# A hybrid decoder layer: low parts of the last head on GpSimd, and the level of 16 block by block

## The chip, the cores and the metric

The kernel runs on one core of one Trainium2 chip. The metric is the device time of one execution in microseconds (us). A core has five engines with an instruction queue each: TensorE (PE, matrix multiplies; its weight loads are shown apart as PEld), VectorE (DVE), ScalarE (ACT), GpSimd (POOL) and SyncE (SP, which here issues the DMA transfers). The engines work at the same time and wait for one another through semaphores; each takes its own instructions in the order in which they stand. Operands lie in SBUF, the on-chip memory of 128 partitions; matrix products land in PSUM, eight banks of 512 float32 columns.

## The reference, cut to what matters

One decoder layer over 2048 tokens of width 1024: a normed projection feeds four heads of a gated linear recurrence (HGRN2) and eight heads of sliding-window attention; both are joined by an output projection, and a gated MLP follows. All is float32.

```python
u = rmsnorm(h, norm_mix_w[l])
proj = u @ w_in[l]
...
f = lb + (1.0 - lb) * jax.nn.sigmoid(hf.astype(jnp.float32))
...
    scores = jnp.einsum('bhtk,bhsk,bhtsk->bhts', qi, ki, decay)
    intra = jnp.einsum('bhts,bhsv->bhtv', scores, vi)
...
m = jnp.maximum(jnp.max(scores, axis=-1, keepdims=True), sink)
p = jnp.exp(scores - m)
denom = jnp.sum(p, axis=-1, keepdims=True) + jnp.exp(sink - m)
...
mix = jnp.concatenate([o_hg, o_att], axis=-1)
h = h + mix @ w_out[l]
```

## The kernel before

**Products in three parts.** A float32 operand x is kept as a high part (a cast to float32r by ACT) and a low part (x minus the high part, one subtraction with two SBUF inputs). A product is then high by high, high by low and low by high: three PE instructions. `split` (line 214) makes the parts of an activation tile, XH and XL; `prep` (line 177) loads a weight tile and makes whi and wlo; `unit` (line 190) multiplies a weight tile with eight activation tiles over two blocks of 512 tokens, 48 matrix instructions. Before the change ACT makes every high part and DVE every low part.

**Stages.** The 2048 tokens go in two halves of 1024. In each half four rounds (`h` = 0 to 3, line 1106 on) run one head of the recurrence (`hgrn`, line 433) and two heads of attention (`attend`, line 343) side by side. Then come the output projection (`out_proj`, line 641), the gate and up products and the down projection. This study is about the last round (`h` = 3) of each half, called **the last head** here. It has no projections of other heads left to fill PE. In their place the output projection already begins: while the last head's recurrence and attention are computed, the mix tiles 0, 4, 1, 5, 2 and 6 (three of the recurrence, `hg` tiles; three of attention, `att` tiles) are split, and the products `pop` of output tiles 0, 1 and 2 run with the six tiles that exist; tiles 7 and 3 are this round's own results and come last.

**Attention of the last head.** q (`att` tile 3) is split for two key/value groups and two blocks of 512 tokens: ACT casts qh (lines 359, 360), DVE makes ql (line 361), four times 64x512. PE makes the scores psc, ACT and DVE move and mask them into sc (lines 378 to 381), DVE takes the maximum (384), ACT the exponentials (394), DVE scales (399), PE transposes (ppt, 408), DVE masks (po, pp, 411), PE multiplies with the values (poT, 419).

**The recurrence by levels.** The decayed scores inside a chunk of 128 tokens are built by levels m = 1, 2, 4, ... 64: at each level PE multiplies K and Q (plev), DVE multiplies Q and K by the decays f (lines 522, 523) for the next level, and the level's scores are placed in the matrix ST. A level therefore waits for the one before it: plev, then Q and K, then the next plev. For m below 32 the last head computes a level as eight products of a whole chunk (line 515) of which the wanted blocks are picked by a predicated copy with a mask on DVE (line 538); for m = 32 and 64 each block is a small product of its own (line 520) and ACT copies it into place (line 543). After the last level come the transposes pkn, the state updates pu and SS, and the outputs po. In the round before, `hgrn` ends with a chain of tiny DVE instructions of 128x8 (lines 158 to 168, an inverse square root) that feeds the scaling `on` (587), PE's transposes pot (592), the product with the gate (593) and the next head's PSUM banks; this chain of the third head falls into the beginning of the last head.

**Order.** Instructions are not issued as the code is written: a scheduler at build time lays all engines' instructions out in order of its own estimate of time, so a change of one duration or engine reorders the neighbours. The order of each engine is then fixed; on the chip only waits move things. GpSimd has nothing to do before the change but the masks at the start. The pools that matter: PSUM has two banks of the kind `hg` (plev, pot, pdiag, pkn, pu, po) and two of `at` (psc, ppt, poT).

Of the kernel before, what the change touches and what calls it, by code (L numbers as in the profile page):

```python
# [8 lines left out]
F32 = mybir.dt.float32  # L9
# [4 lines left out]
ALU = mybir.AluOpType  # L14
# [4 lines left out]
D = 1024  # L19
# [6 lines left out]
HG = 4  # L26
ATT_J = 4
# [22 lines left out]
def hymba_layer(ctx: ExitStack, tc: tile.TileContext, a: dict, out: bass.AP):  # L50
    nc = tc.nc
# [122 lines left out]
            nc.sync.dma_start(t, src)  # L174
        return t

    def prep(src, slots=False, parts=(slice(0, D),), between=[]):

        raw = raw4(None)
        hi, lo = [hp.tile([P, D], F32R, tag="m", name=f"w{t}", bufs=KT) if slots else  # L180
                  wp.tile([P, D], F32R, tag=t, name=f"w{t}", bufs=2) for t in ("hi", "lo")]
        for c in parts:
            nc.sync.dma_start(raw[:, c], src[:, c])
            nc.scalar.copy(hi[:, c], raw[:, c])  # L184
            nc.vector.tensor_tensor(lo[:, c], raw[:, c], hi[:, c].bitcast(F32), op=ALU.subtract)  # L185
            if between:
                between.pop(0)()
        return hi, lo
# [26 lines left out]
    def split(src, w=None, eng=None, dst=None):  # L215

        h, l = dst or new_x()
        if w is None:
            nc.scalar.copy(h, src)
            (eng or nc.vector).tensor_tensor(l, src, h.bitcast(F32), op=ALU.subtract)  # L220
        else:
            nc.scalar.activation(h, src, AF.Identity, scale=w)
            nc.vector.scalar_tensor_tensor(l, src, w, h.bitcast(F32), op0=ALU.mult, op1=ALU.subtract)
        return h, l
# [118 lines left out]
    def attend(hf, j, X, invb, KS, V, mix, p):  # L343
# [8 lines left out]
        for g in range(NB):  # L352
            sc = p.tile([P, 2, 4, P], F32, tag="sc", name="sc", bufs=2)
            gs = slice(g * 512, (g + 1) * 512)
            for kv in range(2):
                r, other = rows(kv), rows(1 - kv)

                qh, ql = [p.tile([P, 512], F32R, tag="pp", name=n, bufs=4) for n in ("qh", "ql")]
                nc.scalar.copy(qh[r], qT[r, gs])
                nc.scalar.copy(qh[other], qT[r, gs])  # L360
                nc.vector.tensor_tensor(ql[r], qT[r, gs], qh[r].bitcast(F32), op=ALU.subtract)
                nc.scalar.copy(ql[other], ql[r].bitcast(F32))
                for i0 in (0, 2):
                    pb = ps("at", "psc")
                    first = hf == 0 and g == 0 and i0 == 0
                    for i in range(2):
                        n = g * 4 + i0 + i
                        w0 = 1 if first and i == 0 else 0
                        o = pb[:, i * 256 + w0 * P:(i + 1) * 256]
                        ks = slice((n + w0) * P, (n + 2) * P)  # L370
                        for t, qx in enumerate((qh, ql)):
                            nc.tensor.matmul(o, qx[:, (i0 + i) * P:(i0 + i + 1) * P], KS[:, kv, ks],
                                             start=t == 0, stop=t == 1)
                    pv = pb.rearrange("p (i w k) -> p i w k", i=2, w=2)
                    dst = sc[:, kv, i0:i0 + 2]
                    if first:
                        nc.vector.memset(dst[:, 0], NEG)
                        nc.scalar.copy(dst[:, 1], pv[:, 1, 0])
                    else:
                        nc.scalar.copy(dst, pv[:, :, 0])  # L380
                    nc.vector.copy_predicated(
                        dst, C.own.bitcast(U32).unsqueeze(1).to_broadcast([P, 2, P]), pv[:, :, 1])
            m = p.tile([P, 2, 4], F32, tag="mx", name="m", bufs=2)
            nc.vector.tensor_reduce(m.rearrange("p a b -> p (a b)"),
                                    sc.rearrange("p a b c -> p (a b) c"), axis=AX.X, op=ALU.max)
            sk = C.sinkb[:, j].unsqueeze(2).to_broadcast([P, 2, 4])
            nc.vector.tensor_tensor(m, m, sk, op=ALU.max)
            es = p.tile([P, 2, 4], F32, tag="es", name="es", bufs=2)
            nc.vector.tensor_tensor(es, sk, m, op=ALU.subtract)
            nc.vector.tensor_scalar(m, m, -1.0, None, op0=ALU.mult)  # L390
            den = p.tile([P, 2, 4], F32, tag="den", name="den", bufs=2)
            for kv in range(2):
                for i in range(4):
                    nc.scalar.activation(sc[:, kv, i], sc[:, kv, i], AF.Exp, bias=m[:, kv, i:i + 1],
                                         accum_out=den[:, kv, i:i + 1])
            nc.scalar.activation(es, es, AF.Exp)
            nc.vector.tensor_tensor(den, den, es, op=ALU.add)
            nc.vector.reciprocal(den, den)
            nc.vector.tensor_tensor(sc, sc, den.unsqueeze(3).to_broadcast([P, 2, 4, P]), op=ALU.mult)
            scs.append(sc)  # L400
# [32 lines left out]
    def hgrn(hf, h, X, invb, vs, WG, mix, p, fu=None):  # L433
# [51 lines left out]
        def place_pairs():  # L485
# [14 lines left out]
            ov = odd[r].rearrange("p r (b m) -> p r b m", m=m)  # L500
            return lambda: nc.vector.copy_predicated(STv[r, :, 1, :, 1], mk[r], ov)

        for m in LEVELS:
            nb = HALF // (2 * m)
            nbc = 64 // m
            Qv = Q.rearrange("p (b w m) -> p b w m", w=2, m=m)
            Kv = K.rearrange("p (b w m) -> p b w m", w=2, m=m)
            Fv = F.rearrange("p (b w) -> p b w", w=2)
            pl = ps("hg", "plev")
            paired = m < 32 and h < HG - 1  # L510
            if paired:
                pairs()
            elif m < 32:
                for c in range(TT):
                    marks[m] = nc.tensor.matmul(pl[:, c * 64:(c + 1) * 64], K[:, c * P:(c + 1) * P],
                                                Qv[:, c * nbc:(c + 1) * nbc, 1], start=True, stop=True)
            else:
                for c in range(TT):
                    for s0 in range(0, P, 2 * m):
                        nc.tensor.matmul(pl[s0:s0 + m, c * m:(c + 1) * m], K[:, c * P + s0:c * P + s0 + m],  # L520
                                         Q[:, c * P + s0 + m:c * P + s0 + 2 * m], start=True, stop=True)
            nc.vector.tensor_tensor(Qv[:, :, 1], Qv[:, :, 1], Fv[:, :, 0:1].to_broadcast([P, nb, m]), op=ALU.mult)
            done = nc.vector.tensor_tensor(Kv[:, :, 0], Kv[:, :, 0], Fv[:, :, 1:2].to_broadcast([P, nb, m]), op=ALU.mult)
            if left:
                with tc.issue_after(done.ins):
                    left()
                left = None
            if m < 64:
                nc.vector.tensor_tensor(Fv[:, :, 0], Fv[:, :, 0], Fv[:, :, 1], op=ALU.mult)
                F = Fv[:, :, 0]  # L530
            else:
                F = p.tile([P, nb], F32, tag="F", name="F", bufs=2)
                nc.vector.tensor_tensor(F, Fv[:, :, 0], Fv[:, :, 1], op=ALU.mult)
            if paired:
                left = place_pairs()
            elif m < 32:
                mk = C.lmask[m].bitcast(U32).rearrange("p (b m) -> p b m", m=m)
                nc.vector.copy_predicated(ST.rearrange("p c (b w m) -> p c b w m", w=2, m=m)[:, :, :, 1],
                                          mk.unsqueeze(1).to_broadcast([P, TT, nbc, m]),
                                          pl.rearrange("p (c b m) -> p c b m", c=TT, m=m))  # L540
            else:
                for s0 in range(0, P, 2 * m):
                    nc.scalar.copy(ST[s0:s0 + m, :, s0 + m:s0 + 2 * m],
                                   pl[s0:s0 + m, 0:TT * m].rearrange("p (c m) -> p c m", c=TT))
# [101 lines left out]
    def out_proj(hf, M, p):  # L646
# [6 lines left out]
        ops = Operands(p)  # L653
        ops.get("B11", 0)
        kept, v = [], []
        W = [prep(a["w_out"][d], d == 2) for d in range(3)]
        first = None
        xs = []
        for d in range(KT):
# [443 lines left out]
    for hf in range(NH):  # L1103
        X, kv, invb, rs, f0 = nxt
        with ExitStack() as st:
# [5 lines left out]
            for h in range(HG):  # L1111
# [3 lines left out]
                if h == HG - 1:  # L1115
                    next(at)
                    next(hg)
                    for kt in (0, 4, 1, 5, 2, 6):
                        M[kt] = split(mix[kt])
                    next(hg)  # L1120
                elif h % 2 == 0:
                    next(at)
                    wv = [prep(a["w_v"][h // 2, s]) for s in range(2)]
                    next(hg)
                    vs += project_v(hf, wv, X, rs, p)
                else:
                    next(hg)
                    next(at)
# [80 lines left out]
```

## Time and profile before

| what | value |
|---|---|
| median of 3 runs | 2201.75 us (2201.37 to 2201.8) |
| the profiled execution | 2201.32 us, of it the span 2199.6 us |
| mean granted clock of PE in it | 0.996 of full speed |
| last head, first half | about 322 to 408 us of the span |
| last head, second half | about 1410 to 1497 us of the span |

The profile is one execution. Its page gives the busy time of each engine, the span in 40 slices, the chain of waits that ended last, and groups of equal instructions with their mean duration. Further views used here are: busy time in chosen stretches of the span ("windows"), who waited for whom, the timeline (one row for each instruction, or for a run of equal ones), and the groups with different shapes kept apart. In a row `out<-in` names the tiles, then the shape; xN counts instructions. A PE matrix instruction on float32 operands shows as two records, so eight products are x16. A duration of PE reaches from start to the end that the profiler models, and successive ones overlap, so the start of one to the start of the next tells the rate.

### The profile page before, as it was taken

The page shows a single profiled execution, that of the slowest core. Times are in us where ns is not written, and L with a number is a line of the kernel's source. Part 1 is how long each engine was busy: PE and PEld are TensorE (multiplying, and loading weights), DVE is VectorE, ACT ScalarE, POOL GpSimd, SP SyncE. Part 2 cuts the span into 40 slices and gives each one's busy share as a digit, 9 for nine tenths or more (in the row PEclk, how much of TensorE's full clock was granted, in tenths as well). Part 3 has the DMA queues.
Part 4 walks back from the last instruction along what each step waited for, and adds up shares of the span by engine and source line. Part 5 has one row for each costly group of instructions (what it writes and reads, how often), then busy time and mean ns, then how long its engine had stood idle before and what let it go on. Part 6 is the DMA issues. An engine that isn't in the chain of part 4 may idle for free.

```text
span 2199.6 us, 29514 instructions
## 1 busy us (share of the span) xinstructions
PE 2176.4 (99%) x11406; PEld 1831.2 (83%) x11406; DVE 1643.6 (75%) x2490; ACT 1050.3 (48%) x1845; POOL 6.3 (0%) x27
## 2 busy tenths in 40 slices
PE   9999999999999999999999999999999999999998
PEld 7988988888888888888889889888888888888887
DVE  6568568688887888875856666577888888887766
ACT  5446454454444445335725455535634444444353
POOL 1000000000000000000000000000000000000000
PEclk9999999999999999999999999999999999999999
DMA  4101112323333234964631111204132323259643
GB/s 154 51 30 50 37 44 68 119 73 104 102 111 106 91 125 144 377 235 162 202 125 49 37 37 50 68 30 139 53 134 87 127 84 120 96 190 392 225 136 130
DMA packets 94214, 257.91 MB, mean 117 GB/s; under 512 B 11578, under 2 KB 17402, under 8 KB 94074
## 3 DMA queue, kind: packets, MB, share of 16 engines
q1 hardware_dynamic: 88128, 251.70, 33.5%
q10 hardware_dynamic: 5946, 4.34, 0.7%
q8 instruction: 89, 1.46, 0.3%
q14 instruction: 51, 0.42, 0.1%
HBM read 195.10 MB, written 57.15 MB: 115 GB/s over the span
## 4 chain that ended last, share of the span: by engine, by line
PE 95%; DVE 3%; DMA 1%; ACT 1%; issue 0%; ACTq 0%; DVEq 0%
PE X L790 7%; PE X L791 7%; PE X L792 7%; PE pop L208 7%; PE hq L208 4%; PE q L208 4%; PE f L208 4%; PE g L208 4%; PE pdx L1001 4%; PE pdx L1003 4%; PE Y L792 4%; PE Y L791 4%; PE Y L790 4%; PE pdx L1002 4%; PE pdy L1003 3%; PE pdy L1001 3%
## 5 line engine op out<-in xcount | busy, mean ns | idle before, releaser
L619 ACT CAST whi<-raw 128x1024 fp32r<-128x1024 f32 x88 | 92.7, 1053 | 109.8 <-PE X L791 67.6
L790 PE MATMUL X<-T,whi 128*128 128x512 f32 x352 | 136.9, 389 | 0.0
L791 PE MATMUL X<-T,whi 128*128 128x512 f32 x352 | 136.9, 389 | 0.0
L792 PE MATMUL X<-T,wlo 128*128 128x512 f32 x352 | 136.9, 389 | 0.0
L885 DVE SCALAR_TENSOR_TENSOR y<-ga,cw,y 128x1024 f32<-128x1024 f32 x88 | 112.4, 1279 | 26.0 <-ACT y L883 25.9
L797 ACT COPY u<-X 128x512 f32<-128x512 f32 x88 | 51.5, 585 | 133.8 <-PE X L792 133.7
L620 DVE TENSOR_TENSOR wlo<-raw,whi 128x1024 fp32r<-128x1024 f32 x88 | 107.1, 1217 | 0.0
L184 ACT CAST whi<-raw 128x1024 fp32r<-128x1024 f32 (+2 forms) x61 | 62.7, 1033 | 81.9 <-PE q L208 31.9
L620 DVE TENSOR_TENSOR xld<-raw,xhd 128x1024 fp32r<-128x1024 f32 x72 | 80.7, 1131 | 19.0 <-ACT xhd L619 18.6
L619 ACT CAST xhd<-raw 128x1024 fp32r<-128x1024 f32 x72 | 69.7, 978 | 42.8 <-DMA raw<-act0T 15.3
L208 PE MATMUL pop<-XL,whi 128*128 128x512 f32 x256 | 85.3, 393 | 2.1 <-DVE XL L220 2.1
L208 PE MATMUL pop<-XH,wlo 128*128 128x512 f32 x256 | 84.6, 391 | 0.8 <-DVE wlo L185 0.8
L208 PE MATMUL pop<-XH,whi 128*128 128x512 f32 x256 | 83.9, 395 | 0.2
L185 DVE TENSOR_TENSOR wlo<-raw,whi 128x1024 fp32r<-128x1024 f32 (+2 forms) x61 | 73.1, 1204 | 8.9 <-ACT whi L184 8.9
L792 PEld LDWEIGHTS X<-T,wlo 128*128 128x128 f32 x352 | 66.1, 188 | 13.7
L791 PEld LDWEIGHTS X<-T,whi 128*128 128x128 f32 x352 | 66.1, 188 | 13.8
L790 PEld LDWEIGHTS X<-T,whi 128*128 128x128 f32 x352 | 66.1, 188 | 13.7
L1001 PE MATMUL pdx<-xhd,hid 128*128 128x512 f32 x192 | 74.4, 391 | 1.2 <-ACT hid L619 1.0
L1002 PE MATMUL pdx<-xld,hid 128*128 128x512 f32 x192 | 74.7, 389 | 0.0
L1003 PE MATMUL pdx<-xhd,lod 128*128 128x512 f32 x192 | 73.7, 389 | 0.0
L611 PE MATMUL pvv<-whi,XH 128*128 128x256 f32 x256 | 73.5, 288 | 0.0
L612 PE MATMUL pvv<-whi,XL 128*128 128x256 f32 x256 | 72.7, 285 | 0.0
(363 smaller groups left out, 6560.8 us busy)
## 6 DMA issues: line engine op xcount, KB each, us to landing
wr<-in_w_down SPq DMA_DIRECT2D x90, 512.0 KB, 5.3
raw<-in_w_gate SPq DMA_DIRECT2D x44, 512.0 KB, 3.6
raw<-in_w_up SPq DMA_DIRECT2D x44, 512.0 KB, 3.6
raw<-act0T SPq DMA_DIRECT2D x20, 512.0 KB, 5.8
raw<-act1T SPq DMA_DIRECT2D x20, 512.0 KB, 10.2
act0B<-y SPq DMA_DIRECT2D x33, 256.0 KB, 2.5
act1B<-y SPq DMA_DIRECT2D x33, 256.0 KB, 2.4
raw<-in_w_out SPq DMA_DIRECT2D x16, 512.0 KB, 4.8
```

The lines of the kernel that those rows point to most:

```text
L185: nc.vector.tensor_tensor(lo[:, c], raw[:, c], hi[:, c].bitcast(F32), op=ALU.subtract)
L208: nc.tensor.matmul(o[b], w, x[:, bs], start=f, stop=l)
L611: nc.tensor.matmul(o[:, 0:256], xh[:, t], hi[:, c], start=kt == 0, stop=False)
L619: return (nc.scalar.copy(h, src), (eng or nc.vector).tensor_tensor(l, src, h.bitcast(F32), op=ALU.subtract))
L620: (eng or nc.vector).tensor_tensor(l, src, h.bitcast(F32), op=ALU.subtract))
L790: nc.tensor.matmul(o, wh[:, ws], xh, start=i == 0 and not more, stop=False, skip_group_check=more)
L791: nc.tensor.matmul(o, wh[:, ws], xl, start=False, stop=False, skip_group_check=more)
L792: r = nc.tensor.matmul(o, wl[:, ws], xh, start=False, stop=i == 3, skip_group_check=more)
L885: nc.vector.scalar_tensor_tensor(y, g[:, w:w + HALF], C.cw[:, ft, w:w + 1], y, op0=ALU.mult, op1=ALU.add)
L1001: nc.tensor.matmul(o, wh[:, i, c], ah[:, i, cols], start=f, stop=False, skip_group_check=more)
L1002: nc.tensor.matmul(o, wh[:, i, c], al[:, i, cols], start=False, stop=False, skip_group_check=more)
L1003: nc.tensor.matmul(o, wl[:, i, c], ah[:, i, cols], start=False, stop=l, skip_group_check=more)
```

## The change

Five edits, all in effect only in the last head or in the first weight tiles of the output projection, in both halves:

- the low part ql of the last head's q goes from DVE to GpSimd (4 times 64x512 in a half);
- the low parts of the mix tiles 4, 5 and 6, the three of attention, go to GpSimd (3 times 128x1024); tiles 0, 1 and 2 stay on DVE;
- the low parts of the weights of output tiles 1 and 2 go to GpSimd (2 times 128x1024);
- `prep` takes the engine as a parameter for that;
- level m = 16 of the last head's recurrence is computed as 32 small products of 16 columns, placed by four copies of ACT, where eight chunk products and one predicated copy of DVE stood.

```diff
-    def prep(src, slots=False, parts=(slice(0, D),), between=[]):
+    def prep(src, slots=False, parts=(slice(0, D),), between=[], eng=nc.vector):
...
-            nc.vector.tensor_tensor(lo[:, c], raw[:, c], hi[:, c].bitcast(F32), op=ALU.subtract)
+            eng.tensor_tensor(lo[:, c], raw[:, c], hi[:, c].bitcast(F32), op=ALU.subtract)
...
-                nc.vector.tensor_tensor(ql[r], qT[r, gs], qh[r].bitcast(F32), op=ALU.subtract)
+                eng = nc.gpsimd if j == ATT_J - 1 else nc.vector
+                eng.tensor_tensor(ql[r], qT[r, gs], qh[r].bitcast(F32), op=ALU.subtract)
...
+        blocks = 16 if h == HG - 1 else 32
...
-            elif m < 32:
+            elif m < blocks:
                 for c in range(TT):
                     marks[m] = nc.tensor.matmul(pl[:, c * 64:(c + 1) * 64], K[:, c * P:(c + 1) * P],
...
-            elif m < 32:
+            elif m < blocks:
                 mk = C.lmask[m].bitcast(U32).rearrange("p (b m) -> p b m", m=m)
...
-        W = [prep(a["w_out"][d], d == 2) for d in range(3)]
+        W = [prep(a["w_out"][d], d == 2, eng=nc.gpsimd if d else nc.vector) for d in range(3)]
...
-                        M[kt] = split(mix[kt])
+                        M[kt] = split(mix[kt], eng=nc.vector if kt < 4 else nc.gpsimd)
```

Three lines are added, so the lines behind the level loop stand three further down in the changed program (the plev products of single blocks at 523 in place of 520, the chunk products at 518, the copies of ACT at 546), and between them and `attend` one further down (the predicated copy of the scores at 382).

GpSimd has eighteen new instructions, nine in each half. In the first half they stand in its queue in this order (wlo is a weight's low part, XL that of a mix tile, ql that of q):

```order
L362 TENSOR_TENSOR ql<-att_3032,qh 64x512 x2
L220 TENSOR_TENSOR XL<-att_589,XH 128x1024
L185 TENSOR_TENSOR wlo<-raw,whi 128x1024
L220 TENSOR_TENSOR XL<-att_1614,XH 128x1024
L185 TENSOR_TENSOR wlo<-raw,whi 128x1024
L362 TENSOR_TENSOR ql<-att_3032,qh 64x512 x2
L220 TENSOR_TENSOR XL<-att_2141,XH 128x1024
```

Before, all of these stood in DVE's queue between other work; on GpSimd they have the queue to themselves.

On DVE the moved instructions leave the chain of tiny instructions at the beginning of the last head. In the second half it read, before:

```order
L158 TENSOR_SCALAR ms<-ss 128x8
L220 TENSOR_TENSOR XL<-att_9491,XH 128x1024
L161 TENSOR_SCALAR y<-ms 128x8
L361 TENSOR_TENSOR ql<-att_11934,qh 64x512
L162 TENSOR_SCALAR y<-y 128x8
L163 TENSOR_SCALAR ms<-ms 128x8
L220 TENSOR_TENSOR XL<-hg_10322,XH 128x1024
L166 TENSOR_TENSOR t<-y 128x8
L185 TENSOR_TENSOR wlo<-raw,whi 128x1024
L167 TENSOR_TENSOR t<-t,ms 128x8
L220 TENSOR_TENSOR XL<-att_10516,XH 128x1024
L168 SCALAR_TENSOR_TENSOR y<-t,y 128x8
```

And with the change, from the same first row to the scaling `on` that the chain feeds:

```order
L158 TENSOR_SCALAR ms<-ss 128x8
L161 TENSOR_SCALAR y<-ms 128x8
L162 TENSOR_SCALAR y<-y 128x8
L163 TENSOR_SCALAR ms<-ms 128x8
L166 TENSOR_TENSOR t<-y 128x8
L167 TENSOR_TENSOR t<-t,ms 128x8
...
L167 TENSOR_TENSOR t<-t,ms 128x8
L220 TENSOR_TENSOR XL<-hg_10349,XH 128x1024
L168 SCALAR_TENSOR_TENSOR y<-t,y 128x8
L590 TENSOR_TENSOR on<-po,y 128x512 x2
```

One low part of 1024 columns (of the mix tile 1) is left inside the chain; before, five such and one of ql stood between its first and its last instruction.

On PE the end of the last head is laid out anew. In the first half it read, before, from level 32 to level 64:

```order
L520 MATMUL plev<-Q,K 32x32 x16
L419 MATMUL poT<-po,V 64x128
L419 MATMUL poT<-pp,V 64x128 x2
L419 MATMUL poT<-po,V 64x128 x2
...
L419 MATMUL poT<-pp,V 64x128 x2
L520 MATMUL plev<-Q,K 64x64 x8
```

And with the change, from level 16 to the first of the state updates:

```order
L523 MATMUL plev<-Q,K 16x16 x32
L208 MATMUL pop_3588<-XH,whi 128x512
L208 MATMUL pop_3657<-XH,whi 128x512
...
L523 MATMUL plev<-Q,K 32x32 x16
L523 MATMUL plev<-Q,K 64x64 x8
L409 MATMUL ppt<-ident,sc 128x128 x8
L556 MATMUL pkn<-ident,K 128x128 x8
L420 MATMUL poT<-po,V 64x128 x2
L420 MATMUL poT<-pp,V 64x128
L563 MATMUL pu<-v,Kn 128x128 x4
```

Level 64 now follows level 32 directly, and the second group of attention (ppt, poT), which stood between the levels, comes behind them. On ACT the four new copies stand there in the middle of that group's exponentials:

```order
L395 ACTIVATE sc,den<-sc,m 128x128 x3
L546 COPY ST<-plev 16x8x16 x4
L395 ACTIVATE sc,den<-sc,m 128x128 x5
L546 COPY ST<-plev 32x8x32 x2
L546 COPY ST<-plev 64x8x64
```

Before, the eight exponentials followed each other.

## The prediction

> **What bounds the kernel now.** I read the engines' busy time and the chain of waits on the page first, then the windows of the two stretches that the change touches.
>
> ```profile
> PE 2176.4 (99%) x11406; PEld 1831.2 (83%) x11406; DVE 1643.6 (75%) x2490; ACT 1050.3 (48%) x1845; POOL 6.3 (0%) x27
> PE 95%; DVE 3%; DMA 1%; ACT 1%; issue 0%; ACTq 0%; DVEq 0%
> 322.00:345.00 23.00, 23.00 (x127) 19.82 (x126) 18.26 (x34) 17.68 (x34) 0.00 (x0) 1.00 0.37 115
> 345.00:382.00 37.00, 34.89 (x289) 29.26 (x288) 35.07 (x64) 14.94 (x48) 0.00 (x0) 1.00 0.14 43
> 1432.00:1471.00 39.00, 36.10 (x292) 30.77 (x291) 34.30 (x64) 15.69 (x50) 0.00 (x0) 0.96 0.13 41
> ```
>
> A window row gives the stretch, its length, then the busy time of PE, PEld, DVE, ACT and POOL, the granted clock of PE, and the DMA. PE is the bound of the program as a whole, and DVE holds 3% of the chain. In 345 to 382 us, the last head of the first half, it is otherwise: DVE is busy 35.07 of 37 us and PE misses 2.1; in the second half PE misses 2.9 of 39 us and has a clock of 0.96. Before 345 us PE is full. So the change can give back only PE time that is lost in these two stretches. Who took it is in the view of waits, once for each stretch, and the rows that follow place the large ones of the second half:
>
> ```profile
> PE pop L208 <- DVE XL L220: 0.7, 1, 0.7
> PE plev L515 <- DVE K L523: 0.7, 1, 0.7
> PE pdiag L457 <- DVE hg L593: 0.3, 1, 0.3
> PE poT L419 <- DVE pp L411: 0.2, 1, 0.2
> ...
> PE plev L515 <- DVE K L523: 1.4, 1, 1.4
> PE pop L208 <- DVE XL L220: 1.4, 1, 1.4
> 1437.60 1.22 DVE L220 TENSOR_TENSOR XL<-att,XH 128x1024 fp32r<-128x1024 f32 x1
> 1437.73 0.73 PE L208 MATMUL pop<-XL,whi 128*128 128x512 f32 x2 [1.39 <-DVE XL L220]
> 1454.83 1.98 PE L515 MATMUL plev<-Q,K 128*128 128x64 f32 x16 [1.41 <-DVE K L523]
> 1457.40:1460.00 2.60, 2.60 (x27) 2.33 (x26) 2.55 (x6) 0.00 (x0) 0.00 (x0) 0.50 0.02 6
> ```
>
> All of PE's listed waits are for DVE: 1.9 us in the first half, 2.8 in the second. Right behind the second stall of 1.41 us the clock stands at 0.50, which no stall of the first half brought about.
>
> **The change part by part.** What leaves DVE, by groups (the two numbers behind the bar are all their busy time in us and the mean ns of one):
>
> ```profile
> L361 DVE TENSOR_TENSOR ql<-att,qh 64x512 fp32r<-64x512 f32 x32 | 21.9, 685 | 3.7 <-ACT qh L359 3.3
> L220 DVE TENSOR_TENSOR XL<-att,XH 128x1024 fp32r<-128x1024 f32 x6 | 7.3, 1218 | 0.8 <-ACT XH L219 0.8
> L185 DVE TENSOR_TENSOR wlo<-raw,whi 128x1024 fp32r<-128x1024 f32 x59 | 71.7, 1222 | 7.2 <-ACT whi L184 7.2
> L538 DVE COPY_PREDICATED ST<-lmask,plev x10: 694/712/1314, 354.6 to 1464.2; 128x512 f32<-128x512 uint32 x10
> ```
>
> In each half 4 x 0.685 + 3 x 1.218 + 2 x 1.222 + 0.71 (the median; the copies of 1.3 us are those of levels 1 and 2) = 9.5 us of DVE. Most of it, the ql, the weights and two of the mix tiles, lies where PE is full and DVE is not; there it pays only through what follows earlier on DVE.
>
> What GpSimd takes for it no row shows; its own rows are
>
> ```profile
> L118 POOL MEMSET lmask<- 128x64 f32 x5 | 0.7, 151 | 0.0
> L86 POOL TENSOR_SCALAR_AFFINE_SELECT ident<-ident 128x128 f32<-128x128 f32 x1 | 0.3, 292 | 0.0
> L121 POOL TENSOR_SCALAR_AFFINE_SELECT lmask<-lmask 128x64 f32<-128x64 f32 x5 | 2.3, 487 | 0.0
> 324.96 0.61 ACT L359 CAST qh<-att 64x512 fp32r<-64x512 f32 x1
> 335.22 1.05 ACT L184 CAST whi<-raw 128x1024 fp32r<-128x1024 f32 x1 [0.41 <-PE g L208]
> 346.68 1.05 ACT L219 CAST XH<-att 128x1024 fp32r<-128x1024 f32 x1
> 350.92 1.21 DVE L220 TENSOR_TENSOR XL<-att,XH 128x1024 fp32r<-128x1024 f32 x1
> ```
>
> A lower bound for 1024 columns is DVE's own 1.2 us; a flat select that reads and writes, 0.292 us for 128 columns, gives 2.3; the select with a broken-up pattern, 0.487 for 64, gives 7.8. A subtraction of flat tiles is nearest the flat select: I take 2.3, and 1.2 for ql. [...] GpSimd's queue of the first half then holds 4 x 1.2 + 5 x 2.3 = 16.3 us. Its first input is there at 325.6; the second weight's at 336.3; its last, the cast of mix tile 6, at 347.7, so that XL of tile 6 is ready at 350.0, where DVE had it at 352.1. Everything earlier in the queue is done by 345. At 2.3 us no product waits for GpSimd; at 7.8 us the queue is 54 us long and PE waits for it.
>
> Where the stalls go. With ql and XL out of DVE's row the levels begin earlier. The wait of pop for XL (0.7 and 1.4) ends, since GpSimd delivers 2 us earlier; pdiag's 0.3 ends too, since ql no longer stands between the two L593; the waits of the levels for K (0.7 and 1.4) and of poT (0.2) end if DVE is ahead: -4.7 us. If the second half's stalls go, so should the dip of the clock: (1 - 0.96) x 39 = 1.6 us.
>
> Level 16 itself:
>
> ```profile
> 372.17 2.00 PE L515 MATMUL plev<-Q,K 128*128 128x64 f32 x16
> 376.35 0.70 PE L520 MATMUL plev<-Q,K 128*32 128x32 f32 x32
> L543 ACT COPY ST<-plev 32x256 f32<-32x256 f32 x16 | 5.8, 362 | 11.3 <-PE plev L520 9.6 <-DVE ST L501 1.6
> 360.43 0.60 DVE K L523
> ```
>
> Eight chunk products take 2.0 us. 32 blocks are 64 records; at level 32's pace, 0.70/32 = 22 ns, 1.4 us; should a record cost no less than a chunk's 125 ns, 8. Each record has half the columns of level 32's, so I take 1.4 to 1.6, a gain of 0.3 in each half with the last record's end: -0.6. The four copies cost ACT under 4 x 0.362 = 1.4 us; ACT is busy 14.94 of 37 us and has room, but in the first half they stand in front of five exponentials of the second group, which then wait for level 16.
>
> New waits. In the first half level 64 follows level 32 on PE with nothing between, and DVE makes Q and K between them, 0.60 us each by the chain's row: +1.2 us, uncovered, where poT products filled it. Behind it ppt waits for the exponentials held up by the copies; between 0 and the five of them, 5 x 0.4 = 2.0; since DVE has Q and K of two levels to make meanwhile (2.4 us) I take 0.8.
>
> The sum: -4.7 - 1.6 - 0.6 + 1.2 + 0.8 = -4.9 us. Against the profiled execution's 2201.32 this is 2196.4; the median of the runs lies 0.43 above that execution, so the forecast is **2196.9 us**, 0.22% faster. What a measurement of this kernel can tell from no change is about 0.2%, 4.4 us.
>
> **The rivals.**
>
> *Nothing is gained in the first half, and the clock dips as before.* There the second group of attention, ppt and poT, now stands behind level 64, before pkn and pu; the work that used to be hidden between the levels is only moved. For it speaks that DVE and PE alternate in the chain from level to level whatever DVE is rid of; against it that 9.5 us of DVE are gone from a stretch where DVE is 95% busy. What stays is the second half's 2.8, and 0.3 for level 16: -3.1, or 2198.7; with one of its two stalls left, 2200.1. Both count as no change.
>
> *GpSimd and DVE get in each other's way: slower.* Place: the tiny chain that feeds pot.
>
> ```profile
> 336.20 0.16 DVE L158 TENSOR_SCALAR ms<-ss 128x8 f32<-128x8 f32 x1
> 336.40 0.63 PE L208 MATMUL pop<-XH,whi 128*128 128x512 f32 x2
> 340.72 1.29 DVE L587 TENSOR_TENSOR on<-po,y 128x512 f32<-128x512 f32 x2
> 342.80 1.04 PE L592 MATMUL pot<-ident,on 128*128 128x128 f32 x8
> 1414.76 1.22 DVE L220 TENSOR_TENSOR XL<-hg,XH 128x1024 fp32r<-128x1024 f32 x1
> 1416.50 0.15 DVE L158 TENSOR_SCALAR ms<-ss 128x8 f32<-128x8 f32 x1
> 1422.27 0.40 PE L372 MATMUL psc<-KS,qh 128*128 128x256 f32 x2
> 1426.22 1.27 DVE L587 TENSOR_TENSOR on<-po,y 128x512 f32<-128x512 f32 x2
> 1429.18 1.03 PE L592 MATMUL pot<-ident,on 128*128 128x128 f32 x8
> ```
>
> Nine of its thirteen instructions of 128x8 read two SBUF tiles, as GpSimd's subtractions do. If an instruction of the one waits out the other's, each tiny one can wait 2.3 us. First half: without the weight and the ql (1.8 us) that stood in it the chain ends at 340.2, and pot's place on PE comes behind 24 products of 0.228 from 336.4 and four score products of 0.12, at 342.3: a slack of 2.1; two instructions of 2.3 us and one of 1.2 in between make 5.8, a stall of 3.7. Second half: pot is moved ahead of some twenty products; from 1422.3 only eight score products of 0.12 and four of 0.228 stand before it, so its place is 1424.2. Free of the moved work the chain starts behind the XL of 1414.76, at 1415.9, and thirteen tiny ones of 0.2, one XL of 1.2 and `on` of 1.3 end it at 1421.0, slack 3.2; four of 2.3 and one of 1.2 in between make 10.4, a stall of 7.2. With the gains kept: 2201.75 - 4.9 + 10.9 = 2207.8; with half of those instructions in between, stalls of 0.8 and 2.0, 2199.7. It decides for slower from 9.3 us of such stall. [...] No row here shows it, since GpSimd is idle after the masks. Against it as a full loss: DVE's tiny instructions follow each other 0.2 us apart, and GpSimd's inputs come spaced by ACT's casts, so not each finds one of GpSimd's ahead of it. GpSimd at 7.8 us for 1024 columns belongs here too; it would cost tens of us, and I give it little.
>
> That the change does not do what it says is ruled out by the order: the instructions stand on GpSimd, and level 16 in blocks.
>
> **How the numbers follow.** The forecast, with stalls mostly gone: 0.43. No change: 0.25. Slower: 0.32, since the place of pot in the second half has little slack and nothing bounds the blocking but GpSimd's queue. So faster by over 0.2% 0.43, within 0.2% 0.25, slower by over 0.2% 0.32. The forecast's own range is 2193 to 2199. If all of PE's loss in both stretches went with no new wait it would be 2201.75 - 6.9 = 2194.9; below 2193 I leave 0.08. Upward the range reaches to the blocked case, 2208, and leaves 0.12 above it: 2193 to 2208.
>
> **What would show it.** GpSimd's rows at about 2.3 and 1.2 us; the waits of pop and plev for DVE's XL and K gone from both stretches, and a clock of 1.00 in the second. Level 16 as 64 records in 1.4 to 1.6 us; a PE wait of about 1 us between levels 32 and 64 of the first half. Wrong would make it: rows of GpSimd at 3 us and more, DVE's instructions of 128x8 with a mean well above 0.17 us, a wait of pot for `on` or of PE for POOL, or stalls of the levels that stay although DVE's work is gone.

## The result, and the profile after

| | before | after |
|---|---|---|
| median (six runs each) | 2201.28 us (2199.97 to 2201.8) | 2215.85 us (2212.14 to 2216.22) |
| ratio | 1 | 1.0065, 95% interval 1.0054 to 1.0076 |
| profiled execution, of it the span | 2201.32 us, 2199.6 us | 2216.22 us, 2214.5 us |

The change makes the kernel 0.65% slower: 14.6 us, three times what was hoped for, with the other sign. The time lies outside the range on record.

The busy time and the two last heads of after, as pages and windows show them (a window row: the stretch, its length, busy time of PE, PEld, DVE, ACT and POOL, granted clock, DMA):

```profile
PE 2179.6 (98%) x11502; PEld 1832.3 (83%) x11502; DVE 1645.7 (74%) x2470; ACT 1052.6 (48%) x1853; POOL 43.2 (2%) x45
```

```profile
322.00:345.00 23.00, 19.78 (x100) 16.63 (x99) 17.07 (x22) 15.54 (x28) 15.32 (x7) 0.96 0.37 115
345.00:382.00 37.00, 33.76 (x299) 28.64 (x298) 30.19 (x56) 16.37 (x53) 3.66 (x2) 0.93 0.14 43
1432.00:1471.00 39.00, 31.32 (x182) 27.20 (x180) 30.52 (x51) 15.32 (x42) 9.69 (x6) 0.87 0.28 95
```

Twenty instructions have left DVE, and yet it is busy 2.1 us longer than the 1643.6 of before. PE misses 3.2 us before 345 us, where it was full, and 7.7 of 39 us in the second half (2.9 before); its clock fell in all three stretches. The view of waits, once for each half, names what PE waited for:

```profile
PE psc L373 <- DVE t L166: 3.2, 1, 3.2
PE plev L523 <- DVE f L532: 1.5, 1, 1.5
PE pop L208 <- DVE XL L220: 1.4, 1, 1.4
PE ppt L409 <- DVE sc L400: 0.7, 1, 0.7
...
PE pot L595 <- DVE on L590: 7.4, 1, 7.4
```

The largest is new: pot waits 7.4 us for `on`, at the end of the tiny chain. The timelines of DVE, GpSimd and PE from there, second half (start, duration, engine, instruction):

```profile
1423.58 2.33 DVE L220 TENSOR_TENSOR XL<-hg,XH 128x1024 fp32r<-128x1024 f32 x1
1425.83 2.37 DVE L158 TENSOR_SCALAR ms<-ss 128x8 f32<-128x8 f32 x1
...
1428.45 1.16 DVE L162 TENSOR_SCALAR y<-y 128x8 int32<-128x8 int32 x1
...
1429.84 2.26 DVE L167 TENSOR_TENSOR t<-t,ms 128x8 f32<-128x8 f32 x1
1432.13 2.29 DVE L168 SCALAR_TENSOR_TENSOR y<-t,y 128x8 f32<-128x8 f32 x1
1434.46 2.26 DVE L166 TENSOR_TENSOR t<-y 128x8 f32<-128x8 f32 x1
1436.75 1.19 DVE L167 TENSOR_TENSOR t<-t,ms 128x8 f32<-128x8 f32 x1
...
1439.79 1.29 DVE L590 TENSOR_TENSOR on<-po,y 128x512 f32<-128x512 f32 x2
...
1425.30 2.87 POOL L220 TENSOR_TENSOR XL<-att,XH 128x1024 fp32r<-128x1024 f32 x1 [0.48 <-ACT XH L219]
1428.25 1.32 POOL L362 TENSOR_TENSOR ql<-att,qh 64x512 fp32r<-64x512 f32 x1
1429.65 2.42 POOL L185 TENSOR_TENSOR wlo<-raw,whi 128x1024 fp32r<-128x1024 f32 x1
1432.03 2.36 POOL L220 TENSOR_TENSOR XL<-att,XH 128x1024 fp32r<-128x1024 f32 x1
1434.35 2.34 POOL L185 TENSOR_TENSOR wlo<-raw,whi 128x1024 fp32r<-128x1024 f32 x1
1436.65 1.26 POOL L362 TENSOR_TENSOR ql<-att,qh 64x512 fp32r<-64x512 f32 x1
...
1440.53 1.97 PE L595 MATMUL pot<-ident,on 128*128 128x128 f32 x8 [7.42 <-DVE on L590]
```

Put the two queues side by side and add start and duration. The L167 of 1429.84 ends at 1432.10, GpSimd's wlo of 1429.65 at 1432.07; the L168 of 1432.13 at 1434.42, GpSimd's XL at 1434.39; so for each of the six. A DVE instruction of 0.17 us takes as long as what is left of GpSimd's, and from 1429.84 on DVE gets one tiny instruction through for each of GpSimd's. It holds the other way too: GpSimd's XL of 1425.30 takes 2.87 where others take 2.36, and DVE's XL before it ends at 1425.91. DVE's 128x8 rows are counted as busy while they wait, which is why DVE looks busier with less to do.

In the first half the same chain is held up (L158 and L161 2.3 us each, and ahead of them the Q of 333.04, 3.42 us where 1.22 is usual), but pot is not what suffers: a masked copy of the scores stands in the middle of the chain on DVE.

```profile
336.38 2.37 DVE L158 TENSOR_SCALAR ms<-ss 128x8 f32<-128x8 f32 x1
338.78 2.32 DVE L161 TENSOR_SCALAR y<-ms 128x8 int32<-128x8 int32 x1
...
343.44 0.43 DVE L382 COPY_PREDICATED sc<-own,psc 128x256 f32<-128x256 uint32 x1
...
343.92 0.47 PE L373 MATMUL psc<-KS,qh 128*128 128x128 f32 x1 [3.22 <-DVE t L166]
...
354.18 2.47 DVE L220 TENSOR_TENSOR XL<-hg,XH 128x1024 fp32r<-128x1024 f32 x1
...
353.18 2.39 POOL L220 TENSOR_TENSOR XL<-att,XH 128x1024 fp32r<-128x1024 f32 x1 [1.93 <-ACT XH L219]
...
356.71 0.73 PE L208 MATMUL pop<-XL,whi 128*128 128x512 f32 x2 [1.39 <-DVE XL L220]
```

The copy ends at 343.87 and the next scores start 0.05 us later; the row names t of L166, which ended last before them, but psc does not read it, and the copy is the likelier releaser. The other three rows are one more collision: pop waits 1.39 us for an XL that DVE makes in 2.47 instead of 1.22, because GpSimd began one of its own a microsecond earlier.

The stalls have an echo in PE's clock. Windows of 3 us, from the stall of 3.22 us in the first half, from the waits around level 64, and from the stall of 7.42:

```profile
343.00:346.00 3.00, 2.08 (x7) 1.89 (x8) 2.83 (x11) 0.27 (x1) 0.00 (x0) 0.52 0.30 119
346.00:349.00 3.00, 3.00 (x14) 2.70 (x14) 1.49 (x3) 0.00 (x0) 0.00 (x0) 0.50 0.00 0
349.00:352.00 3.00, 3.00 (x23) 2.92 (x23) 1.23 (x3) 2.72 (x6) 1.27 (x1) 0.84 0.00 0
382.00:385.00 3.00, 2.22 (x22) 2.12 (x23) 2.86 (x8) 1.44 (x5) 0.00 (x0) 0.85 0.00 0
385.00:388.00 3.00, 3.00 (x19) 2.50 (x17) 2.44 (x5) 1.14 (x2) 0.00 (x0) 0.58 0.00 0
...
1440.00:1443.00 3.00, 2.47 (x10) 2.37 (x11) 2.64 (x5) 0.00 (x0) 0.00 (x0) 0.50 0.69 243
1443.00:1446.00 3.00, 3.00 (x9) 2.30 (x9) 1.87 (x3) 1.99 (x2) 0.61 (x1) 0.56 0.99 369
```

The lowest of these windows show 0.50; I read a value between 0.50 and 1.00 as a mix of the two, so that 0.84 over 3 us is 1 us at half speed. By this estimate, from 343.92 PE works at half speed for about 6 us, around 385 us for 3.4 (0.9 and 2.5), from 1440.53 for 5: half of these 14.4 us, 7.2, are lost although PE is busy. The run with level 16 in blocks alone (below) has the same 11,502 PE instructions, a span of 2196.0 and 2172.4 us of PE; after has 2214.5 and 2179.6. Of the 18.5 us between these two profiles 11.3 are idle time of PE, and the remaining 7.2, by which PE is busy longer with the same instructions, agree with the estimate from the windows. (The medians of the two kernels differ by 16.3 us; the account is of these two executions.)

Not all of it stands beside a row of GpSimd. Around level 64 PE waits 1.5 and 0.7 us and then loses half of 3.4 us, 3.9 us in all, and GpSimd's last row of this half ended at 355.57:

```profile
382.12 1.12 PE L523 MATMUL plev<-Q,K 128*64 128x64 f32 x16 [1.48 <-DVE f L532]
```

This part is the new order of PE, level 64 directly behind level 32.

### The profile page after: what moved, and what is told of

Read it like the earlier page. It is cut to its first block, busy times and chain, and to the rows that moved or that the text cites. A ratio compares the mean times of both kernels' runs of the same rounds, so it can differ in the third digit from the quotient of the medians.

```text
span 2214.5 us, 29724 instructions
## 1 busy us (share of the span) xinstructions
PE 2179.6 (98%) x11502; PEld 1832.3 (83%) x11502; DVE 1645.7 (74%) x2470; ACT 1052.6 (48%) x1853; POOL 43.2 (2%) x45
## 4 chain that ended last, share of the span: by engine, by line
PE 93%; DVE 4%; ACT 2%; DMA 1%; issue 0%; ACTq 0%; DVEq 0%
PE X L793 7%; PE X L794 7%; PE X L795 7%; PE pop L208 7%; PE hq L208 4%; PE f L208 4%; PE q L208 4%; PE Y L795 4%; PE Y L793 4%; PE Y L794 4%; PE pdx L1004 3%; PE pdx L1006 3%; PE pdx L1005 3%; PE g L208 3%; PE pdy L1005 3%; PE pdy L1004 3%
## 5 line engine op out<-in xcount | busy, mean ns | idle before, releaser
L185 DVE TENSOR_TENSOR wlo<-raw,whi 128x1024 fp32r<-128x1024 f32 (+2 forms) x57 | 68.2, 1202 | 8.8 <-ACT whi L184 8.8
```

## The experiments

Three theories were tested. A: GpSimd's subtractions and DVE's instructions exclude each other, and what waits in DVE's queue pays. B: the order of the changed program (pot and the scores placed earlier, level 16 in other pieces) is what costs. C: GpSimd is only late with what it delivers. Times are medians, each beside the kernel before on the same chip (2200.4 to 2201.2 us).

### All of the change but level 16, and level 16 alone

```diff
-        blocks = 16 if h == HG - 1 else 32
+        blocks = 32
```

> All of the change but level 16: the GpSimd subtractions alone. Theory A (GpSimd's subtractions and DVE's instructions exclude each other, and the chain of 128x8 instructions ahead of pot and the ql ahead of the scores pay for it): nearly all of the loss of after, 2212 to 2217 us, PE again waiting 6 to 8 us for on in the second half. Theory B (the loss comes from level 16 in blocks and from its copies on ACT): 2199 to 2203.

Measured 2215.75 us, ratio 1.0066 (1.0050 to 1.0081), and pot waits 7.4 us for `on` again. The moved subtractions, with the order that they bring, carry the whole loss; level 64 follows level 32 here too and waits 1.5 us. Level 16 alone (the changed kernel with all subtractions back on DVE) ran twice:

> Level 16 of the last head in blocks, nothing on GpSimd, level 64 of the first half still behind other PE work as in before. All theories but one: little happens, 2200 to 2202.5 us beside 2201.3 for before. The theory that the blocks themselves cost (64 records and four copies in place of 8 products and one masked copy): 2204 or more, with gaps of PE between level 16 and level 32.

> Level 16 in blocks alone, once more, to tell 0.9992 from no change: 0.9985 to 0.9998 if the gain of two stretches of about 0.6 us and of the masked copy is real, 1.000 if not.

Measured 2199.57 and 2199.05 us, ratios 0.9992 (0.9984 to 1.0001) and 0.9991 (0.9982 to 1.0000). The two agree on a gain of 1.6 to 1.7 us; neither interval excludes no change by itself. The groups of this kernel show what became shorter on PE (before, 160 chunk records took 19.3 us):

```profile
L518 PE MATMUL plev<-Q,K 128*128 128x64 f32 x128 | 15.4, 273 | 0.7 <-DVE K L526 0.7
L523 PE MATMUL plev<-Q,K 128*16 128x16 f32 x128 | 1.4, 179 | 0.0
```

19.3 - 15.4 - 1.4 = 2.5 us less of PE in the two halves.

### The work of GpSimd without its results

The kernel before, in which GpSimd repeats five subtractions of each half, in place, into tiles that nobody reads again:

```diff
             nc.vector.tensor_tensor(lo[:, c], raw[:, c], hi[:, c].bitcast(F32), op=ALU.subtract)
+            if again:
+                nc.gpsimd.tensor_tensor(raw[:, c], raw[:, c], hi[:, c].bitcast(F32), op=ALU.subtract)
...
                         M[kt] = split(mix[kt])
+                        if kt >= 4:
+                            nc.gpsimd.tensor_tensor(mix[kt], mix[kt], M[kt][0].bitcast(F32), op=ALU.subtract)
```

> DVE keeps all of its work, in the order of before; GpSimd repeats five of the subtractions of each half (mix tiles 4 to 6, weights 1 and 2) into tiles that nobody reads again, about 2.4 us each. Nothing waits for their results. Theory A (exclusion): slower although no data depend on GpSimd, 2203 to 2211 us, and DVE's instructions that meet a GpSimd row end with it, at 2 us and more. Rival B (the new order of the program, pot and the scores placed earlier, is what costs) and rival C (GpSimd is merely late with what it delivers): 2201 to 2202, and no DVE instruction of 128x8 with a mean above 180 ns.

Measured 2220.79 us, ratio 1.0091 (1.0077 to 1.0105): the slowest of all, with nothing waiting for GpSimd's results and DVE in the order of before, but for four instructions of the first half that stand one or two places earlier. The timelines of GpSimd and DVE in its first half:

```profile
340.20 3.34 POOL L1123 TENSOR_TENSOR att<-att,XH 128x1024 f32<-128x1024 f32 x1 [1.16 <-DVE ms L158]
...
341.25 2.31 DVE L161 TENSOR_SCALAR y<-ms 128x8 int32<-128x8 int32 x1
```

The L161 ends with GpSimd's row (343.56 and 343.54); in the second half the L168 of 1434.27, with two SBUF inputs, takes 2.37 us and ends with GpSimd's row of 1433.22 (1436.64 and 1436.62). So A alone is enough for a loss of this size, without a new order (B) or late data (C). It is larger than expected, and larger than that of after, in a kernel where DVE keeps all of its own 1024-column work beside GpSimd's. The same kernel with two memsets in place of each extra subtraction:

```diff
-                nc.gpsimd.tensor_tensor(raw[:, c], raw[:, c], hi[:, c].bitcast(F32), op=ALU.subtract)
+                [nc.gpsimd.memset(raw[:, c], 0.0) for _ in range(2)]
```

> As extra_sub, but in each place GpSimd clears the same 128x1024 tile twice, so that it writes SBUF for some time and reads nothing. If any access of GpSimd to SBUF holds DVE up: slower, like extra_sub in proportion to the rows' lengths, 2202 to 2209 us. If only instructions of GpSimd that read do (theory A as the prediction stated it): 2201 to 2202 us and no stretched DVE instruction.

Measured 2201.13 us, ratio 1.0000 (0.9991 to 1.0009), with GpSimd at work for 19.2 us and DVE's instructions in the order of the run with subtractions. Writing alone is not what costs. Nor is it the buffers that come free later: in both runs the DMA queue waits ten times for GpSimd to be done with one (45.3 us with the subtractions, 32.8 with the memsets), and none of PE's listed waits in the two last heads is for a load in either. But one half of the expectation failed, as GpSimd's and DVE's timelines show:

```profile
334.17 1.97 POOL L187 MEMSET raw<- 128x1024 f32 x2 [1.07 <-DVE wlo L185]
336.44 1.97 POOL L1123 MEMSET att<- 128x1024 f32 x2 [0.30 <-DVE XL L222]
...
334.02 1.22 DVE L451 TENSOR_TENSOR Q<-hg,f 128x1024 f32<-128x1024 f32 x1
335.16 1.22 DVE L222 TENSOR_TENSOR XL<-att,XH 128x1024 fp32r<-128x1024 f32 x1
...
337.50 0.93 DVE L161 TENSOR_SCALAR y<-ms 128x8 int32<-128x8 int32 x1
```

DVE's instructions with two SBUF inputs (Q, XL) keep their 1.22 us beside a memset. The L161, with one input, ends at 338.43, as the memset does (338.41): it waits even for a write.

### The change without GpSimd's reads

The changed kernel, where GpSimd clears its input and then the low part's tile at each of its nine places (for prep; split and ql alike), so that these low parts are zero:

```diff
-            eng.tensor_tensor(lo[:, c], raw[:, c], hi[:, c].bitcast(F32), op=ALU.subtract)
+            if eng is nc.gpsimd:
+                [eng.memset(t, 0.0) for t in (raw[:, c], lo[:, c].bitcast(F32))]
+            else:
+                eng.tensor_tensor(lo[:, c], raw[:, c], hi[:, c].bitcast(F32), op=ALU.subtract)
```

> The changed kernel with one thing taken away: in each of its nine places of a half, GpSimd clears its input tile and then the low part's tile instead of subtracting (two writes, no read, about 1.9 us together for 1024 columns), so that it works in the same places and nearly as long. The low parts are zero then. 90 to 100 of PE's 9,581 rows stand elsewhere than in after. Theory A (exclusion by GpSimd's reads): the stalls of pot and of the scores are gone, and the gains that the prediction hoped for come through, 2194 to 2200 us. Rival B (the new order) and rival C (what GpSimd makes comes late): still 2208 to 2216, with PE waiting for on or for the scores' operands.

Measured 2196.22 us, ratio 0.9979 (0.9970 to 0.9988): 4.2 us faster than before, and within 0.7 us of the forecast on record. Its waits (first and second half), windows and chain:

```profile
PE plev L527 <- DVE K L535: 0.7, 1, 0.7
...
PE plev L527 <- DVE K L535: 0.6, 1, 0.6
```

```profile
345.00:382.00 37.00, 35.53 (x354) 30.06 (x354) 32.56 (x62) 16.23 (x53) 1.13 (x2) 1.00 0.15 44
1432.00:1471.00 39.00, 37.21 (x365) 31.31 (x364) 31.23 (x63) 14.25 (x51) 0.00 (x0) 1.00 0.07 23
```

```profile
1415.30 0.17 DVE L158 TENSOR_SCALAR ms<-ss 128x8 f32<-128x8 f32 x1 [1.43 <-ACT on L592]
...
1419.31 1.29 DVE L599 TENSOR_TENSOR on<-po,y 128x512 f32<-128x512 f32 x2
...
1423.18 1.03 PE L604 MATMUL pot<-ident,on 128*128 128x128 f32 x8
```

The same chain, 15.3 us long in after (1425.83 to 1441.08), is 5.3 long here (1415.30 to 1420.60), and pot starts 2.6 us behind its end without waiting. So most of the new order does no harm by itself, and rival B does not explain the loss. But this run does not have the order of after in one place: in its first half the poT products of the second group stand between levels 32 and 64 again, so it says nothing of the 3.9 us around level 64. The run with q on GpSimd and level 16 in blocks (below) happens to have that order in its second half, with GpSimd idle since 1434.67: level 64 waits 1.48 us for f at 1464.93, ppt 0.56 behind it, and the clock is 0.50 from 1467 to 1470 us. That piece is B's, and these losses are about what they are in after, though that run as a whole is no slower than before (2200.21 us). A cleared tile does not wait for the cast, so this run alone would not exclude C; the extra subtractions above do.

One input in place of two, GpSimd copying the high part:

> As after, but GpSimd copies the high part into the low part's tile instead of subtracting: one SBUF input in place of two. If any read of GpSimd holds DVE: rows of GpSimd at half to all of their length, DVE's 128x8 instructions still ending with them, 2203 to 2214 us. If only GpSimd's instructions of two inputs do: 2195 to 2200 us, and no DVE instruction stretched.

Measured 2201.24 us, ratio 1.0003 (0.9994 to 1.0013), between the two expectations. Reads of one input do hold DVE's instructions with two, by their own, shorter time (a cast of 128x1024 by itself takes 1.04 us; timelines of GpSimd and DVE):

```profile
1420.82 1.93 POOL L186 CAST wlo<-whi 128x1024 fp32r<-128x1024 f32 x1 [1.61 <-ACT whi L184]
...
1421.75 1.01 DVE L168 SCALAR_TENSOR_TENSOR y<-t,y 128x8 f32<-128x8 f32 x1
```

They end at 1422.75 and 1422.76. pot does not wait any more. The order is another again, with one large stall that after does not have (pop, 3.1 us for a cast of ACT), so its total is no price for one input.

### Smaller pieces

Each of GpSimd's subtractions cut into pieces of 256 columns:

```diff
-            eng.tensor_tensor(lo[:, c], raw[:, c], hi[:, c].bitcast(F32), op=ALU.subtract)
+            for s in ([slice(i, i + 256) for i in range(0, D, 256)] if eng is nc.gpsimd else [c]):
+                eng.tensor_tensor(lo[:, s], raw[:, s], hi[:, s].bitcast(F32), op=ALU.subtract)
```

> The changed kernel with each of GpSimd's subtractions cut into pieces of 256 columns (four for 1024, two for a ql), some 0.65 us each by 2.39 / 4. If an instruction of DVE waits out one instruction of GpSimd and no more, DVE's stretched 128x8 rows end at 0.7 us instead of 2.3, the stall of pot shrinks from 7.4 to 2 to 4 us, and the time is 2203 to 2211 us. If the block holds for all that is queued on GpSimd, or follows from late data, nothing changes: 2214 to 2218.

Measured 2204.89 us, ratio 1.0021 (1.0011 to 1.0031). DVE's chain in its second half:

```profile
1419.23 3.50 DVE L158 TENSOR_SCALAR ms<-ss 128x8 f32<-128x8 f32 x1
...
1425.12 0.66 DVE L166 TENSOR_TENSOR t<-y 128x8 f32<-128x8 f32 x1
...
1426.51 0.66 DVE L168 SCALAR_TENSOR_TENSOR y<-t,y 128x8 f32<-128x8 f32 x1
```

The block is per instruction, as expected: the held rows of 128x8 take 0.6 to 0.7 us, the chain is 13.0 us long instead of 15.3, pot waits 4.2 instead of 7.4, and the loss falls from 14.6 to 4.1 us. The L158 is the exception: it waits 3.50 us through the last ql piece and four XL pieces in a row. Why it does not get in between them is open.

### Which move costs

Each move alone, and two pairs:

> Only the low parts of the three mix tiles on GpSimd, six instructions of some 2.5 us in all. Theory A: they stand in the middle of the chain of 128x8 instructions of the second half and before the level loop of the first: 2203 to 2211 us. Theory C (GpSimd late): PE waits for XL from GpSimd, 2202 to 2205, no stretched DVE instruction.

> Only the low parts of the weights 1 and 2 on GpSimd, four instructions in all. Theory A: each can cost DVE up to 2.3 us behind it and gives 1.2 back, at the chain's end in both halves: 2200 to 2207 us. Theory C: 2200 to 2202 us, since the weights are wanted late.

> Only the four low parts of q of each half on GpSimd, 1.27 us each. With 4.8 us measured for the mix tiles and 1.3 for the weights alone, 8.4 us are left of after's 14.6 if the three add up: 2209 us. If the loss grows with the number of GpSimd rows that stand together in the chain (an interaction): 2200 to 2204.

> The low parts of the mix tiles and of the weights on GpSimd, q on DVE. If the costs add: 2201 + 4.8 + 1.3 = 2207. If the slack of pot's place is used up once and every further blocked row then stalls PE: 2210 to 2215, with a wait of pot for on of 3 us and more in the second half.

> The low parts of q and of the mix tiles on GpSimd, the weights on DVE. If the costs add: 2201 + 4.8 - 0.7 = 2205. If slack decides: 2207 to 2213, with a wait of pot or of the scores of 2 us and more.

The chain is timed in the second half, from the start of L158 to the end of `on`; pot's place is how far behind the chain's start PE is ready for pot (start of pot less its wait; where it did not wait, at most that).

| on GpSimd | median, ratio | against before | chain | pot's place | pot waits |
|---|---|---|---|---|---|
| nothing (before) | | | 11.0 us | 12.7 | 0 |
| ql | 2200.06, 0.9996 (0.9987 to 1.0005) | -0.7 us | 9.9 | 11.7 | 0 |
| weights | 2201.65, 1.0005 (0.9996 to 1.0015) | +1.3 | 12.0 | 11.2 | 0.2 |
| mix tiles | 2205.20, 1.0021 (1.0012 to 1.0031) | +4.8 | 10.8 | 10.2 | 0 |
| ql, mix tiles | 2206.13, 1.0025 (1.0015 to 1.0034) | +5.1 | 11.2 | 7.3 | 3.4 |
| mix tiles, weights | 2210.67, 1.0047 (1.0034 to 1.0061) | +9.7 | 14.0 | 9.2 | 4.3 |
| all three | 2215.75, 1.0066 (1.0050 to 1.0081) | +14.6 | 15.3 (after) | 7.3 | 7.4 |

The three add up to 5.4 us and cost 14.6 together. Alone, no move makes pot wait 1 us (the weights 0.2 in the second half and 0.6 in the first): some of DVE's own long instructions still stand between the tiny ones, and pot's place is 10 us or more behind the chain's start (the 4.8 us of the mix tiles arise elsewhere: in their second half PE waits 1.8 us for K and has a clock of 0.91 from 1432 to 1471 us). With several moves fewer of DVE's long instructions are left between the tiny ones, and the scheduler, which evidently does not reckon with the exclusion, places pot at 7.3 or 9.2. Each of these differences is uncertain by 2 to 3 us. So the 9.2 us by which all three exceed their sum are clear of noise; the 3.6 us of mix tiles and weights and the 1.0 us of ql and mix tiles are not, and there only pot's waits of 4.3 and 3.4 us speak for an interaction.

### A version that beats both

> A try at a version that keeps what pays: only mix tile 6, whose XL pop waits for, on GpSimd, and level 16 in blocks. If the exclusion costs no more than that XL's wait gives back: 2197 to 2200 us. If GpSimd's 2.4 us again push the row of DVE behind it: 2200 to 2205.

> The low parts of q on GpSimd and level 16 in blocks, the two parts that cost nothing alone. If their small gains add: 2198 to 2199 us, 0.9985 to 0.999 of before; if the exclusion takes the gain: 2200 to 2202.

Measured 2199.08 us, 0.9992 (0.9983 to 1.0001), and 2200.21 us, 0.9996 (0.9988 to 1.0005). Neither is better than level 16 alone. In the first, GpSimd's XL takes 2.4 us and pop still waits for XL, 1.3 and 1.7 us, longer than the 0.7 and 1.4 of before. What stands is level 16 in blocks, worth some 1.6 us if it is real, and nothing on GpSimd.

## Why the prediction was wrong, point by point

**GpSimd's durations: right.** 2.3 and 1.2 us were taken; undisturbed rows show 2.39 (128x1024) and 1.27 (64x512). Held up by DVE they reach 3.4.

**The sum of gains: near the total of a kernel in which nothing excludes, in part by luck.** -4.9 was forecast; the change without GpSimd's reads gives -4.2. In it pop's waits for XL are gone from both halves and PE misses 1.5 and 1.8 us in the two stretches, where it missed 2.1 and 2.9. But the levels still wait 0.7 and 0.6 us for K, which the sum let go entirely, level 16 gains more than it allowed, and the +1.2 and +0.8 of new waits cannot arise there, since poT stands between levels 32 and 64. The errors cancel.

**Level 16: the gain was too small.** 64 records take 0.70 us, not 1.4 to 1.6: a record of 16 columns costs 11 ns, half of one of 32 (22 ns), not as much. With 2.0 us for the chunk products that is 1.25 us in each half, four times the 0.3 of the sum.

**The clock of the second half, -1.6: not founded.** The run with the extra memsets has the same two stalls of 1.4 us and a clock of 1.00 in that stretch; the 0.96 was not set by those stalls alone.

**"The wait of pop for XL (0.7 and 1.4) ends, since GpSimd delivers 2 us earlier": wrong in the first half of after.** There pop waits 1.39 us for another XL, DVE's, which GpSimd's has pushed back (354.18 above).

**Level 64 behind 32, +1.2, and the exponentials, +0.8: about right.** plev L523 waits 1.5 us and ppt 0.7 in the first half. What was left out is that PE's clock goes to half behind them, for 3.4 us, so that 2.0 became 3.9.

**The step that failed is the choice between the forecast and the rival "GpSimd and DVE get in each other's way".** The sum had no term for a DVE instruction that waits for GpSimd's; the rival had it, at the right place, and put the second half's stall at 7.2 us against 7.42. That closeness is partly luck: it counted four rows of 2.3 us and one of 1.2 among the instructions with two inputs, and three of 2.3 and one of 1.2 were held, with the single-input L158 (2.37) and L162 (1.16) beside them, while pot stood 7.3 us behind the chain's start instead of 8.3. The rival was set aside because "GpSimd's inputs come spaced by ACT's casts, so not each finds one of GpSimd's ahead of it". They did not come spaced: from 1429.65 to 1437.91 four of GpSimd's rows follow each other without a gap, and each catches one tiny instruction.

**Three things made the loss 8 us larger than the rival's 2207.8.** It kept all gains, though the same collisions take some of them back (pop's 1.39 us). It had no price for the clock, 7.2 us in the profile. And it took only the nine instructions with two inputs as exposed; the single-input L158, L161 and L162 wait as well, 717, 348 and 335 ns on the mean, where an undisturbed row takes 0.16 us, and the first half's stall came from these and the Q ahead of them, at the scores and not at pot. How much of the 8 us each of the three makes was not measured apart.

That instructions of GpSimd and DVE wait for one another was an assumption of the rival, which no row of before shows. The runs show it, and where it ends: DVE's 128x8 instructions with two inputs took 2.2 to 2.4 us beside GpSimd's 128x1024 subtractions (2.26 to 2.29 in after, 2.19 to 2.37 in the run with extra ones), where 0.17 is usual; beside memsets two-input instructions of 128x1024 kept their 1.22 us, and the single-input L161 took 0.93. The prediction gave all of slower less than even odds, 0.32.

## What to carry to other kernels

Moving a two-input subtraction to an idle GpSimd did not free DVE here: for 1.2 us taken off DVE's queue, up to 2.4 us followed in which DVE's next instruction on SBUF tiles waited, so count a moved instruction as up to GpSimd's length of DVE time, unless DVE is idle then. The worst neighbours were the short DVE instructions in a chain, since each waited out a whole GpSimd instruction (four of 0.17 us in a row took 2.26, 2.29, 2.26 and 1.19); count the pairs, not the microseconds of work. A move that is free alone is no evidence for three of them: time the chain against the place where its result is wanted, and add for each stall of several microseconds the products at half clock behind it (6.0 us of them behind the stall of 3.22, 5.1 behind that of 7.42).

## What the runs showed of the hardware that was not expected

In the first half of the run with extra memsets, single-input instructions of DVE on 128x8 were held up beside GpSimd's memsets, 0.93, 0.84 and 0.78 us (L161, L162, L163) instead of 0.16, while two-input ones of 128x1024 (XL, Q) ran beside them unchanged, 1.22 us. DVE instructions with one input from PSUM were not held up beside a reading GpSimd: `on` (L599) in the run with one input, two instructions in 1.29 us from 1422.80 (1.29 in after too, with GpSimd idle), ran beside a GpSimd cast of 1422.69 to 1423.74.

PE's granted clock went to 0.50 within each of the two large stalls of after: in windows of 1 us it is 1.00 from 342 to 343 and 0.57 from 343 to 344, where PE resumes at 343.92; in the longer stall it is 1.00 from 1434 to 1435, 0.71 in the next window, and 0.50 from 1436 on, with PE idle until 1440.53. Behind the stall of 3.22 us half speed lasted 6.0 us, behind that of 7.42 5.1. Around level 64 no single wait is longer than 1.5 us, and the clock still fell, for 3.4 us; in the run with extra memsets two waits of 1.4 us leave it at 1.00.
